# The steps of an attention pair at other slots of the schedule

## The chip, the cores and the metric

The kernel runs on one core of a Trainium2 chip. A core has five engines that each work through their own queue in order: TensorE (PE in the profile; PEld is its loading of weights), VectorE (DVE), ScalarE (ACT), GpSimd (POOL) and SyncE (SP). SP and POOL issue most of the DMAs. The metric is the time of one execution on the device in microseconds; below, the median of three runs is used, and one further execution was profiled.

## The reference

Two layers, each a mixer with two branches over 256 tokens of 2048 channels, in float32. What matters here is the attention branch and what runs beside it:

```python
proj = h @ w_in                                  # one input projection, cut into nine parts
y_conv = conv_branch(c_a, c_glu, c_gate, ...) @ w_proj_conv    # GLU, causal depthwise conv of width 31, LayerNorm, gates
q  = rmsnorm((rmsnorm(q_down) @ w_uq))           # 16 heads of 128 + 64 (rotary)
kv = rmsnorm(kv_down) @ w_ukv                    # 16 heads: 128 of key, 128 of value
s  = q @ k.T * scale, masked by chunks of 64     # per head, 256 x 256
o  = softmax(s) @ v
y  = sigmoid(g_conv) * y_conv + sigmoid(g_mla) * (o * silu(gate)) @ w_proj_mla
x  = x + y @ w_out
```

## The kernel before

**Products and slots.** Every large product is cut into blocks of at most 512 output columns, and a block runs over its weight pieces of 256 rows. One piece is a *slot*: twelve matmuls (two token halves, two row groups, three terms). Three terms, because a float32 weight is split into a high part, rounded by a cast on ACT (`split_hi`, tile `hi`), and a low part, the difference, taken on DVE (`split_lo`, tile `lo`). Both are made some slots ahead: before the matmuls of slot j come the cast for slot j+3 and the difference for slot j+2. There are 4 buffers for high parts, 3 for low parts, 5 for raw weights, which SP loads in order.

**The order of the work.** Each engine's instructions are issued in the order of the Python program; nothing is reordered. After the matmuls of a slot, `background` (L243) advances a slot counter, then issues the steps that are due (`at_slot(ahead, f, vec, act)` files a step `ahead` slots from now), then *fill* work, and last what the steps appended to `late`. A step's work therefore stands in the DVE and ACT queues between the weight splits of neighbouring slots, and its matmuls stand between the matmuls of neighbouring slots.

**The planner's budget.** Fill is the depthwise convolution, one *tap* after another, on DVE. A tap is either two multiply-adds of 128x256, one for each half (charged 0.81 by the planner), or one add of 128x512 (charged 0.62) if ACT has scaled the input before (`assist`, when ACT's own budget is over 0.8). Each slot earns for DVE what the planner's estimate of the slot leaves beside the low part: 1.55 for a slot of 512 columns, 1.18 for one of 384. Charges of the due steps are taken off, and as long as the balance is above zero a tap is issued; a negative balance is carried on, a positive one is not:

```python
        slot = 12 * (n / 2400 + 0.0133) - 0.04
        for e, split_us in (("vec", KS * n / 960 + 0.06), ("act", KS * n / 1066 + 0.04)):
            budget[e] = min(budget[e], 0.0) + slot - split_us
```

These are the planner's numbers, fixed in the code; they decide only where a tap stands.

**A round.** The attention works on pairs of heads, eight to a layer. For pair b a layer runs two slots of `uq` (384 columns, queries), two of `ukv` (512, keys and values) and eight of another block: a `glu` block (input of the convolution) for pairs 0 to 4, a `cgate` block for pairs 5 and 6. So there is a round of twelve slots from the end of one `ukv` product to the end of the next. Below, *round b* is the one after pair b's `ukv`, and its slots are counted 1 to 12: 1 to 8 are `glu` or `cgate`, 9 and 10 `uq` of the next pair, 11 and 12 its `ukv`.

**The steps of a pair** (`attention`, L667, steps filed at L812 to L825) are counted in slots from the end of its `ukv`, over almost three rounds, so that three pairs are at work in each round. In order: `stats` (DVE, 14 small operations: the RMSNorm factors), `scale_k` (DVE, four operations; then eight DMAs on POOL park the query and key rows in DRAM, `turn_d<-qk`), `back_in("qk")` (two POOL DMAs fetch them back, `qk<-turn_d`), `blockwise` (DVE, two transposes of 32x32 blocks), `split_nope` (three ACT operations; differences on DVE a slot later), `split_rope` (six ACT casts; four differences on DVE a slot later), `scores` (16 matmuls, tile `s`), `maxima` (DVE, after a copy on ACT; tiles `sx`, `nb`), `exponentials` (ACT, into tile `pr`; then four POOL DMAs park it, `turn_d<-pr`), `back_in("p")` (one POOL DMA, `pr<-turn_d`), `turn_p` (DVE: reciprocal, transpose), `split_p` (a cast on ACT, and `late` a difference on DVE, tile `pv`), `values` (12 matmuls, tile `o_ps`), `outputs` (a copy on ACT, `o_sb`). Within a slot, steps are issued in the order in which they were filed, the older pair first.

**Beside them in each round.** The block that ends with slot 8 is evacuated in slot 9: for `glu` two sigmoids on ACT and, as `late`, two products on DVE (tile `su`; then eight POOL DMAs `turn_d<-su`, two fetches four slots on, two transposes `u_t` eight slots on, which open the next block of taps); for `cgate` two silus on ACT and eight parks. The `uq` block is evacuated in slot 11, `ukv` in slot 1 of the next round. `ukv` in slot 11 writes the two PSUM tiles that the `glu` or `cgate` block held, so it can't begin before that evacuation is done. After the last tap of a block comes one more sum (`s1c`).

Of the kernel before, what the change touches and what calls it, by code (L numbers as in the profile page):

```python
# [63 lines left out]
EVAC_AT = 1  # L64
FETCH_AT, TURNED_AT = 4, 8

STATS_AT, SCALE_AT, QK_BACK_AT, QK_TURN_AT, NOPE_AT, ROPE_AT, SCORES_AT = 2, 3, 6, 11, 12, 14, 17
MAX_AT, EXP_AT, P_BACK_AT, P_TURN_AT, P_SPLIT_AT, VALUES_AT, O_AT = 18, 19, 23, 28, 30, 32, 34

REVOLUTION_PIECES = 6  # L70

# [1249 lines left out]
```

## Time and profile before

| | us |
|---|---|
| median of 3 runs (lowest, highest) | 1892.09 (1891.77, 1892.33) |
| the profiled execution, whole time | 1891.51 |
| its span, first to last instruction | 1889.7 |
| PE busy | 1881.9 (100%) |
| DVE busy | 1601.2 (85%) |
| ACT busy | 1331.5 (70%) |
| POOL busy | 392.9 (21%) |

The granted TensorE clock is 1.000. How to read the rows below: a row of instructions has the start and the length in us, the engine, the operation, the tile written and the tiles read, shapes, and how many instructions were merged into the row; in brackets stands how long the engine had been idle before it and what ended that. Instructions of one engine overlap a little at their ends, so a cost in a queue is best taken from start to start. Busy PE is no sign of PE at its peak; a stall of PE shows as a longer distance between matmuls that stand in the same order.

### The profile page before, as it was taken

What the parts mean: (1) busy time and instruction counts of PE and PEld (TensorE: products, weight loads), DVE (VectorE), ACT (ScalarE), POOL (GpSimd) and SP (SyncE); (2) the same over time, 40 slices, a digit from 0 to 9 for tenths busy, and PEclk for the clock granted to TensorE, in tenths of its full rate; (3) what the DMA queues carried; (4) which work ended last, traced back from release to release, by engine and by line L of the source; (5) the groups of instructions that cost most, each with busy time, mean ns of one, the idle gap of its engine ahead of it and who ended that gap; (6) DMA issues with size and microseconds to landing.
All of it is one profiled execution on the core that took longest, in us unless ns stands there. A gap on an engine that the chain in (4) does not pass through costs nothing.

```text
span 1889.7 us, 27378 instructions
## 1 busy us (share of the span) xinstructions
PE 1881.9 (100%) x8744; PEld 1589.4 (84%) x8744; DVE 1601.2 (85%) x2623; ACT 1331.5 (70%) x2350; POOL 392.9 (21%) x734
## 2 busy tenths in 40 slices
PE   9999999999999999999999999999999999999999
PEld 8988888888888888888899888888888888888887
DVE  6899998899999998765679898888999999985654
ACT  7677878878787866544557688688887878474442
POOL 1043433332200000121211443343322000001200
PEclk9999999999999999999999999999999999999999
DMA  9678778776765566677866877787767555666764
GB/s 321 218 251 275 258 236 272 256 256 225 229 210 192 187 218 217 216 236 258 281 209 216 263 263 243 260 266 241 257 228 237 199 189 195 225 213 215 237 224 164
DMA packets 137232, 441.91 MB, mean 234 GB/s; under 512 B 23296, under 2 KB 27136, under 8 KB 137088
## 3 DMA queue, kind: packets, MB, share of 16 engines
q1 hardware_dynamic: 104256, 358.84, 56.5%
q0 software_dynamic: 31968, 80.26, 13.4%
q8 instruction: 68, 1.11, 0.2%
q10 hardware_dynamic: 864, 1.07, 0.2%
q14 instruction: 76, 0.62, 0.1%
HBM read 397.61 MB, written 42.47 MB: 233 GB/s over the span
## 4 chain that ended last, share of the span: by engine, by line
PE 97%; DVE 2%; ACT 1%; DMA 0%; issue 0%; POOL 0%; ACTq 0%; DVEq 0%
PE acc L127 94%; PE s L127 2%; PE o_ps L127 1%; DVE lo L127 1%; DVE v_t L127 0%; DMA x_in<-in_xT 0%; ACT hi L127 0%; ACT tap L127 0%; DVE qk L127 0%; DMA turn_d<-pr 0%; PE tp L127 0%; ACT qk L127 0%; DVE rsq_t L127 0%; DVE ym L127 0%; ACT junk L127 0%
## 5 line engine op out<-in xcount | busy, mean ns | idle before, releaser
L127 ACT CAST hi<-raw 128x1024 fp32r<-128x1024 f32 (+3 forms) x689 | 699.5, 1022 | 411.7 <-PE acc L127 351.7
L127 DVE TENSOR_TENSOR lo<-raw,hi 128x1024 fp32r<-128x1024 f32 (+3 forms) x689 | 811.4, 1181 | 207.8 <-PE acc L127 164.7
L127 PE MATMUL acc<-hi,hT 128*128 128x512 f32 (+2 forms) x1728 | 419.8, 382 | 0.0
L127 PEld LDWEIGHTS acc<-hi,hT 128*128 128x128 f32 x1728 | 319.8, 188 | 59.1
L127 ACT ACTIVATE tap<-u_t,cst 128x256 f32<-128x256 f32 x598 | 260.9, 500 | 14.6 <-DVE v_t L127 13.6
L127 PE MATMUL acc<-hi,h_hi 128*128 128x512 f32 (+2 forms) x864 | 261.3, 384 | 1.1 <-ACT hi L127 1.1
L127 PE MATMUL acc<-hi,h_lo 128*128 128x512 f32 (+2 forms) x864 | 260.1, 382 | 0.0
L127 PE MATMUL acc<-lo,h_hi 128*128 128x512 f32 (+2 forms) x864 | 229.8, 382 | 0.0
L127 PE MATMUL acc<-lo,hT 128*128 128x512 f32 (+2 forms) x864 | 229.3, 382 | 0.0
L127 DVE TENSOR_TENSOR v_t<-v_t,tap 128x512 f32<-128x512 f32 x299 | 205.3, 687 | 10.1
L127 PEld LDWEIGHTS acc<-hi,h_lo 128*128 128x128 f32 x864 | 161.2, 188 | 30.2
L127 PEld LDWEIGHTS acc<-hi,h_hi 128*128 128x128 f32 x864 | 160.4, 188 | 31.0 <-ACT hi L127 1.5
L127 PEld LDWEIGHTS acc<-lo,h_hi 128*128 128x128 f32 x864 | 160.9, 188 | 30.0
L127 PEld LDWEIGHTS acc<-lo,hT 128*128 128x128 f32 x864 | 160.6, 188 | 29.9
L127 POOL DMA_DIRECT2D turn_d<-gate x176 | 95.6, 551 | 321.5 <-DVE gate L127 278.0
L127 DVE SCALAR_TENSOR_TENSOR v_t<-u_t,cst,v_t 128x256 f32<-128x256 f32 x362 | 155.4, 480 | 3.0
L127 POOL DMA_DIRECT2D turned<-turn_d x82 | 45.9, 560 | 519.6 <-DVE v_t L127 317.3
L127 PE MATMUL acc<-hi,oT 128*128 128x512 f32 x512 | 128.1, 390 | 0.0
L127 PE MATMUL acc<-hi,yT 128*128 128x512 f32 x512 | 128.0, 389 | 0.0
L127 PE MATMUL acc<-hi,ycT 128*128 128x512 f32 x512 | 127.8, 389 | 0.0
L127 PE MATMUL acc<-hi,qkc 128*128 128x512 f32 (+1 forms) x512 | 119.0, 364 | 0.2
L127 PEld LDWEIGHTS acc<-hi,oT 128*128 128x128 f32 x512 | 96.1, 188 | 20.1
(171 smaller groups left out, 2139.8 us busy)
## 6 DMA issues: line engine op xcount, KB each, us to landing
raw<-in_win SPq DMA_DIRECT2D x383, 512.0 KB, 4.2
raw<-in_wpm SPq DMA_DIRECT2D x64, 512.0 KB, 3.2
raw<-in_wpc SPq DMA_DIRECT2D x64, 512.0 KB, 4.0
raw<-in_wo SPq DMA_DIRECT2D x64, 512.0 KB, 4.3
raw<-in_wukv SPq DMA_DIRECT2D x32, 512.0 KB, 5.2
turned<-turn_d POOLq DMA_DIRECT2D x50, 256.0 KB, 4.5
raw<-in_win SPq DMA_DIRECT2D x32, 384.0 KB, 4.4
raw<-in_wuq SPq DMA_DIRECT2D x32, 384.0 KB, 3.0
```

Source lines behind the costliest of these rows:

```text
L127: ins = getattr(self.engine, name)(*a, **k)
```

## The change

Only two lines of constants change: the slots of a pair's steps.

```diff
-STATS_AT, SCALE_AT, QK_BACK_AT, QK_TURN_AT, NOPE_AT, ROPE_AT, SCORES_AT = 2, 3, 6, 11, 12, 14, 17
-MAX_AT, EXP_AT, P_BACK_AT, P_TURN_AT, P_SPLIT_AT, VALUES_AT, O_AT = 18, 19, 23, 28, 30, 32, 34
+STATS_AT, SCALE_AT, QK_BACK_AT, QK_TURN_AT, NOPE_AT, ROPE_AT, SCORES_AT = 3, 5, 8, 11, 12, 15, 18
+MAX_AT, EXP_AT, P_BACK_AT, P_TURN_AT, P_SPLIT_AT, VALUES_AT, O_AT = 19, 20, 24, 29, 30, 32, 35
```

In slots of a round (counts above 12 and 24 fall into the next rounds):

| step | slot before | slot after |
|---|---|---|
| `stats` | 2 | 3 |
| `scale_k` and 8 parks | 3 | 5 |
| fetch of the rows, 2 DMAs | 6 | 8 |
| `blockwise`, `split_nope` | 11, 12 | the same |
| `split_rope`, its differences | 2, 3 | 3, 4 |
| `scores` | after 5 | after 6 |
| `maxima` | 6 | 7 |
| `exponentials` and 4 parks | 7 | 8 |
| fetch of `pr` | 11 | 12 |
| `turn_p` | 4 | 5 |
| `split_p`, `values` | 6, 8 | the same |
| `outputs` | 10 | 11 |

No instruction is added or removed; the orders of the queues of PE, DVE, ACT and POOL change, and with the charges the slots in which the planner puts taps.

## The prediction

> **What bounds the kernel now.** I read the page's first part, then PE's waits, then the chain of waits, then the timeline of one attention round, engine by engine. PE is busy throughout, its waits are small, and the chain (start, length, what) runs along PE's products with 16 score matmuls in each round:
>
> ```profile
> PE   1881.9 (100%) x8744; PEld 1589.4 (84%) x8744; DVE 1601.2 (85%) x2623; ACT 1331.5 (70%) x2350; POOL 392.9 (21%) x734
> ...
> PE acc L127 <- ACT hi L127: 1.1, 1, 1.1
> PE s L127 <- DVE qk_t L127: 0.7, 1, 0.7
> ...
> 208.50 1.89 PE s L127 x16
> 243.18 1.89 PE s L127 x16
> 383.12 1.89 PE s L127 x16
> 1147.17 1.89 PE s L127 x16
> 1181.88 0.04 DVEq L127
> 1217.60 2.23 PE s L127 x16
> 1322.80 1.89 PE s L127 x16
> ```
>
> From 208.50 to 243.18 a round takes 34.68 us; I take that as the unstalled round. The four rounds to 383.12 take 139.94, 1.22 more than 4 x 34.68; the five from 1147.17 to 1322.80 take 175.63, 2.23 more. So all stalls of both attention stages come to 3.45 us, and that is all a better order of these steps could give back. But at 1181.88 the chain leaves PE and returns only at 1217.60: for a whole round something other than PE set the pace. It is a loop of DVE and ACT, seen in the timelines of that round (a window with the busy time of PE, PEld, DVE, ACT, POOL; then DVE, then ACT, then PE):
>
> ```profile
> 1158.60:1193.30 34.70, 34.70 (x174) 29.96 (x173) 31.03 (x63) 28.06 (x65) 13.39 (x26) 1.00 0.77 253
> ...
> 1179.88 1.78 DVE L127 TENSOR_TENSOR qk_t<-qk,qk_t 64x256 fp32r<-64x256 f32 x4
> 1188.43 0.16 DVE L127 TENSOR_TENSOR nb<-nb,rs_p 128x4 f32<-128x4 f32 x1
> 1188.51 0.95 DVE L127 TENSOR_TENSOR pv<-pr,pv 128x768 fp32r<-128x768 f32 x1
> 1189.38 1.82 DVE L127 TENSOR_TENSOR lo<-raw,hi 128x768 fp32r<-128x768 f32 x2
> 1191.12 1.41 DVE L127 TENSOR_TENSOR v_t<-v_t,tap 128x512 f32<-128x512 f32 x2
> 1194.23 1.23 DVE L127 TENSOR_TENSOR lo<-raw,hi 128x1024 fp32r<-128x1024 f32 x1 [1.71 <-ACT hi L127]
> 1196.98 0.88 DVE L127 SCALAR_TENSOR_TENSOR su<-acc,rinv_x,su 128x256 f32<-128x256 f32 x2 [1.51 <-ACT su L127]
> 1198.90 1.67 DVE L127 SCALAR_TENSOR_TENSOR v_t<-u_t,cst,v_t 128x256 f32<-128x256 f32 x4
> 1200.60 0.69 DVE L127 TENSOR_TENSOR s1c<-s1c,v_t 128x512 f32<-128x512 f32 x1
> 1202.35 1.83 DVE L127 STREAM_TRANSPOSE qk<-qk 128x768 f32<-128x768 f32 x2
> ...
> 1189.81 1.28 ACT L127 ACT_TABLE_LOAD   x1 [3.30 <-DVE pv L127]
> 1193.07 0.20 ACT L127 ACTIVATION_READ_ACCUMULATOR pr<-s,nb,rs_p 128x1 f32 x1
> 1193.16 1.99 ACT L127 CAST hi<-raw 128x1024 fp32r<-128x1024 f32 x2
> 1195.17 1.28 ACT L127 ACT_TABLE_LOAD   x1
> 1196.47 0.84 ACT L127 ACTIVATE su<-acc,rinv_x 128x256 f32<-128x256 f32 x2
> 1229.04 0.19 ACT L127 ACTIVATION_READ_ACCUMULATOR pr<-s,nb,rs_p 128x1 f32 x1
> ...
> 1197.61 2.09 PE L127 MATMUL acc<-hi,qkc 128*128 128x512 f32 x8
> ```
>
> The reader is to see a ring. DVE's maxima (`nb`) and the difference `pv` release ACT's table load and exponentials; they end at E = 1193.07 + 0.20 = 1193.27. Behind them in ACT's queue stand two casts (1.99), a table load (1.28) and the sigmoids `su`; the first product on DVE is done at about 1197.45, and PE's slot 11, which needs that PSUM tile, starts at 1197.61, E + 4.3. Then DVE works its queue through to the next maxima without a long wait. From E to the next E (1229.23) are 35.96 us; 0.69 of them is the `s1c` sum, which falls into few rounds, so the ring takes 35.27 where PE needs 34.68. It is as good as closed already. DVE is busy 31.03 of 34.70, and most of its idle time is the two waits for ACT just behind the maxima (1.71 and 1.51). What is put ahead of the maxima lengthens the ring; what stands behind them, while ACT works, is free.
>
> **The change part by part.** Seen from the ring, most moves cost nothing: `stats`, `scale_k`, the rotary differences (1.78), `turn_p` and the maxima all stood between the transposes of `qk` and the maxima, and still do. Four things differ.
>
> (a) The difference `pv` (slot 6) used to stand behind the maxima (slot 6) with the exponentials waiting for it; now it stands ahead of them (slot 7). ACT waited for it then, so: nothing.
>
> (b) The maxima stand a slot later, so the low part for slot 9, first half of the pair at 1189.38 (0.87 from start to start), is now ahead of them: +0.87.
>
> (c) Taps. The charges for DVE in slots 1 to 8 were 1.95, 2.2, 2.75, 1.0, 0.8, 2.4, 0, 0, and each slot earns 1.55. A late round of the first layer leaves slot 12 at about -0.45 and goes -0.85, -1.50, -2.70, -2.14, -1.39, -2.24, -0.69 and at slot 8 +0.86: two taps there, two in slot 10. The pair at 1191.12 (1.41) is slot 8's: behind the maxima, free. Now they are 1.95, 0, 2.2, 1.65, 2.9, 0.9, 1.5, 0, and the same walk gives slot 1 -1.0 and slot 2, where no step is left, +0.5: a tap there, ahead of the maxima. It has no ACT help (ACT's budget recovers only in slots 5 to 7), so it costs half of the 1.67 at 1198.90: +0.84. Carried on round by round, the walk gives one tap in slot 2 in rounds 2 to 6 of the first layer; in the second layer one in round 2, two (+1.67) in rounds 3, 5 and 6, and one with `s1c` (0.84 + 0.69) in round 4. Slot 10 gets one or two adds in place of multiply-adds: -0.13 each.
>
> (d) The exponentials stand a slot later, so one cast (half of 1.99) fewer lies between them and `su`: -0.98.
>
> Ring on DVE and ACT alone: 35.27 + 0.87 + 0.84 - 0.98 - 0.13 = 35.87 with one tap, 35.27 + 0.87 + 1.67 - 0.98 - 0.27 = 36.56 with two.
>
> (e) POOL's queue. The rows' fetch moves from slot 6 to slot 8, and there the older pair's four parks of `pr` are filed ahead of it. Before, it waited only for its own parks:
>
> ```profile
> 1185.78 0.57 POOL L127 DMA_DIRECT2D qk<-turn_d  x1 [1.50 <-DMA turn_d<-qk]
> 1189.27 0.56 POOL L127 DMA_DIRECT2D qk<-turn_d  x1 [2.92 <-DMA turn_d<-qk]
> 1193.56 2.20 POOL L127 DMA_DIRECT2D turn_d<-pr  x4 [3.73 <-ACT pr L127]
> ...
> qk<-turn_d POOLq DMA_DIRECT2D x32, 384.0 KB, 5.4
> ...
> DMA to landing us min/median/max: 2.1/3.6/6.9
> ```
>
> Now: E + 0.3, parks 2.20, so the two fetches go out at E + 2.5 and E + 3.1 and land (5.4) at E + 7.9 and E + 8.5. DVE reaches the two transposes (half of 1.83 each) at about E + 7.3 (before: 1202.35, E + 9.1 with 0.69 of `s1c`; now 1.11 earlier by (d) and slot 10) and ends them at E + 9.7 where it would have ended at E + 9.1: +0.6. The ends: 2.1 to landing makes it 0; 6.9 makes the transposes end at E + 11.2: +2.1. I take 0.6, by the median of this very transfer. The ring is then 36.5 with one tap, 37.2 with two; against 34.68 PE stalls 1.8 or 2.5 a round.
>
> [...]
>
> The rest lies beside other work. `scores` moves from a point where the rotary differences end at 1181.66, right at the matmuls, to one slot later, with `scale_k` no longer ahead of them but a low part and a tap or two more. A slot, on average 34.68 / 12 = 2.9 us, is as long as a low part and two taps (1.23 and 1.67), and the four scalings are gone from there besides; so the differences are done in time, and the 3.45 us of old stalls vanish. `outputs` now queues behind the `uq` evacuation; its 0.59 falls into ACT's waiting for the transposes, and were that gone would cost at most 0.59 of ACT, whose 28.06 has room. The fetch of `pr` has five slots to `turn_p` as before. `su`'s parks stand behind the fetch on POOL and have four slots. SP's order is untouched.
>
> **The sum.** In rounds 2 to 6 exponentials stand before an evacuation that slot 11 waits for.
>
> ```profile
> 222.88 0.87 DVE L127 SCALAR_TENSOR_TENSOR su<-acc,rinv_x,su 128x256 f32<-128x256 f32 x2 [1.52 <-ACT su L127]
> ...
> 223.94 2.01 PE L127 MATMUL acc<-hi,qkc 128*128 128x512 f32 x8
> ...
> L127 ACT ACTIVATE gate<-acc,rinv_x 128x512 f32<-128x512 f32 x32 | 20.5, 684 | 0.4 <-DVE v_t L127 0.2
> L127 DVE STREAM_TRANSPOSE u_t<-turned 128x256 f32<-128x256 f32 x32 | 12.2, 420 | 0.0
> L127 ACT COPY o_sb<-o_ps 128x512 f32<-128x512 f32 x16 | 9.4, 588 | 0.0
> ```
>
> Round 2: the first product (half of 0.87) is ready at about 223.35, 0.6 before PE wants it. E comes later by 0.87 + 0.84 and about 0.9 carried over from round 1 (an estimate: that round's own (b) and (c), less DVE's idle time), 2.6; less 0.98 and 0.6 leaves 1.0. Rounds 3 and 4: 1.8 each. Round 5: a `cgate` block, freed by one silu on ACT (0.68) instead of half of `su`'s 0.84 on ACT and then half of 0.87 on DVE, hence about 0.2 to 0.3 earlier: 1.5. Round 6: besides, no `u_t` transposes (2 x 0.42, overlapping, about 0.7), which leaves about 0.4 less again: 1.1. First layer 7.2. Second layer: 1.0, 2.5, 2.4, 2.2, 1.8: 9.9. Together 17.1, less the old 3.45: +13.7. The profiled execution took 1891.5, so 1905.2; the median lies 0.6 above it: 1906. With fetches that never hold DVE, ten rounds lose 0.6 each: 1900. With the worst landing they gain 1.5 each: 1921.
>
> **The rivals.** (1) Faster: the scores stop waiting for the rotary differences and no new wait appears. Place: slot 11. It decides if the exponentials end less than 0.98 + 0.6, about 1.6 us, later, that is if (b) and (c) are swallowed by DVE's 3.2 us of waits. For it: the 0.7 wait of `s` is real. Against: those waits stand behind the maxima, the new work ahead. Time: 1892.1 - 3.45 = 1888.6. (2) No change: the lateness does not add up over rounds, because PE's own slack of 0.6 and the shorter casts take it; each layer loses about what it wins. Against it: the ring of 35.27 shows no slack to recover in. 1890 to 1895. (3) POOL decides: the fetches, back to back behind the parks and beside weight loads, land at 6.9 or later. For it: DMA share 0.77 in the window. 1913 to 1921 or above.
>
> **How the numbers follow.** The forecast, a ring of 36 to 37 us, has 0.72, with a range of its own of 1898 to 1913. Rival 3 has 0.12, rival 2 0.11, rival 1 0.05. Leaving out rival 1, most of rival 2 and the far end of rival 3 gives 1894 to 1919. A measurement of this kernel tells about 0.2% (3.8 us) from no change; rival 1's 3.45 hardly reaches it. Faster 0.05, within it 0.12, slower 0.83.
>
> **What would show it.** In the changed kernel the chain of waits should run through DVE and ACT in rounds 2 to 6 of both layers; score groups 36 to 37.5 us apart; slot 11's first matmul waiting for DVE `su` (in `cgate` rounds ACT `gate`) and the wait of `s` for `qk_t` gone; POOL's `qk` fetch waiting for its parks no longer; DVE's transposes of `qk` waiting for a DMA by about 0.6; a tap of multiply-adds between the `vl` and `stats` work. Wrong would make it: rounds that stay at 34.7 (the ring is not closed), or a fetch that lands far from 5.4.

## The result, and the profile after

The changed kernel takes 1913.62 us (median of four runs, 1913.13 to 1914.98) beside 1892.21 for the kernel before in the same series. The ratio is 1.0113, with a 95% interval of 1.0097 to 1.0129: slower by 21 us. The profiled execution took 1913.8, its span 1911.7, 22.0 more than before, and PE is busy 1888.2 of it. The planner also made three taps of the changed kernel in the other form, two multiply-adds in place of an add that ACT helps: DVE runs 2626 instructions where it ran 2623, ACT 2344 where it ran 2350. So a few instructions do change with the slots.

The waits of the changed kernel (in us: in total, how many, the longest), PE's first, then what DVE waits for ahead of the transposes of `qk` and ahead of the products `su`:

```profile
PE acc L127 <- DVE su L127: 7.4, 6, 2.3
PE acc L127 <- ACT gate L127: 4.9, 4, 1.6
PE acc L127 <- DVE lo L127: 2.2, 4, 0.9
PE acc L127 <- ACT hi L127: 2.0, 1, 2.0
PE s L127 <- DVE qk_t L127: 0.7, 3, 0.2
PE mu L127 <- DVE s1c L127: 0.2, 1, 0.2
...
DVE su L127 <- ACT su L127: 20.7, 8, 4.3
DVE qk L127 <- DMA turn_d<-gate: 13.4, 4, 3.9
DVE qk L127 <- DMA qk<-turn_d: 7.4, 7, 2.7
```

The first six lines come to 17.4 us, where the kernel before had 1.8 (1.1 and 0.7). The 2.0 for `hi` stands at the start of the program, as the 1.1 did before. Most of the rest is slot 11, waiting for the evacuation that frees its PSUM tiles, by `su` in `glu` rounds and by `gate` in `cgate` rounds. The last two lines are new and come to 20.8: DVE stands still because the rows of `qk` have not come back. (The tile in the name of a releasing DMA is the one seen last; the rows themselves are `qk<-turn_d`.)

Round 2 of the first layer in the chain of waits (start, length, what):

```profile
221.28 3.05 PE acc L127 x18
224.33 0.94 ACT hi L127
225.27 0.02 issue
225.29 1.28 ACT L127
226.57 0.01 issue
226.58 0.48 ACT su L127
227.06 0.02 issue
227.09 0.49 DVE su L127
227.58 0.14 issue
227.72 23.64 PE acc L127 x96
```

This is the ring of the prediction, now closed around PE: exponentials end at 224.33, then one cast (0.94), the table load, one sigmoid, one product, and slot 11 at 227.72. The timeline of the same round, POOL, DVE and PE:

```profile
224.62 2.18 POOL L127 DMA_DIRECT2D turn_d<-pr  x4 [4.09 <-ACT pr L127]
226.79 1.12 POOL L127 DMA_DIRECT2D qk<-turn_d  x2
...
222.74 0.68 DVE L127 TENSOR_TENSOR v_t<-v_t,tap 128x512 f32<-128x512 f32 x1
227.09 0.87 DVE L127 SCALAR_TENSOR_TENSOR su<-acc,rinv_x,su 128x256 f32<-128x256 f32 x2 [3.66 <-ACT su L127]
...
227.72 3.65 PE L127 MATMUL acc<-hi,qkc 128*128 128x512 f32 x8 [2.27 <-DVE su L127]
```

POOL parks `pr` 0.3 after the exponentials and fetches the rows at once behind it, as foreseen. DVE idles 3.66 behind the maxima (1.52 before at this place). And the eight matmuls of slot 11 take 3.65, where the same eight took 2.01 before: after the stall PE ran at half its pace for a while, 1.6 us on top of the 2.27. The second layer has the same at 1176.67 (3.63). The named waits (+15.6, of which 0.9 is that at the start of the program) and the two slow stretches (+3.3) make 18.9 of the 22.0; the rest is in shorter distances between matmuls.

### The profile page after: what moved, and what is told of

It is laid out like the page before. It is cut to its first block, busy times and chain, and to the rows that moved or that the text cites. A ratio compares the mean times of both kernels' runs of the same rounds, so it can differ in the third digit from the quotient of the medians.

```text
span 1911.7 us, 27327 instructions
## 1 busy us (share of the span) xinstructions
PE 1888.2 (99%) x8744; PEld 1590.3 (83%) x8744; DVE 1601.7 (84%) x2626; ACT 1324.5 (69%) x2344; POOL 392.2 (21%) x734
## 4 chain that ended last, share of the span: by engine, by line
PE 87%; DVE 5%; issue 2%; ACT 2%; DMA 2%; POOL 1%; ACTq 0%; DVEq 0%
PE acc L127 85%; DVE lo L127 2%; DVE v_t L127 1%; PE s L127 1%; PE o_ps L127 1%; DVE qk_t L127 1%; ACT hi L127 1%; DMA qk<-turn_d 1%; ACT L127 1%; POOL turn_d L127 0%; DMA x_in<-in_xT 0%; DVE qk L127 0%; ACT pr L127 0%; DMA turn_d<-gate 0%; DMA turn_d<-su 0%
## 5 line engine op out<-in xcount | busy, mean ns | idle before, releaser
L127 POOL DMA_DIRECT2D turn_d<-qk x128 | 69.9, 554 | 242.5 <-DVE qk L127 167.9
```

The source lines that it names most:

```text
L127: ins = getattr(self.engine, name)(*a, **k)
```

## The experiments

Every kernel below computes all of the reference unless something else is said. E is the end of a pair's exponentials, as in the prediction.

**One kernel with three moves, one with eight.** First the change was cut in two: the kernel before with the first three moves (factors, scaling, fetch), and the changed kernel with those three taken back.

```diff
 e3_first_three, against the kernel before
-STATS_AT, SCALE_AT, QK_BACK_AT, ... = 2, 3, 6, 11, 12, 14, 17
+STATS_AT, SCALE_AT, QK_BACK_AT, ... = 3, 5, 8, 11, 12, 14, 17
 e4_other_eight, against the changed kernel
-STATS_AT, SCALE_AT, QK_BACK_AT, ... = 3, 5, 8, 11, 12, 15, 18
+STATS_AT, SCALE_AT, QK_BACK_AT, ... = 2, 3, 6, 11, 12, 15, 18
```

> Only the first three moves (factors in the third slot, scaling and its parks in the fifth, rows fetched back in the eighth); all else as before. Taps move to slot 2 by the planner's walk. Theory R: ring 35.27 + 0.84 to 1.67 = 36.1 to 36.9, nothing else changed in it, so as bad as the whole change or nearly: 1904 to 1914. Theory Q: the exponentials and their parks are a slot earlier than the fetch here, so the fetch stands half as long behind them: 1900 to 1906.

> Only the other eight moves (rotary split, scores, maxima, exponentials, fetch of the probabilities, their turn, the outputs a slot later); factors, scaling and the rows' fetch in the second, third and sixth slot as before. By the planner's walk no tap stands ahead of the maxima in rounds 2 to 5. Theory R: ring 35.27 + 0.87 - 0.98 = 35.2 as before, and the scores no longer wait for the rotary differences: 1890 to 1895. Theory Q: the fetch is back ahead of the exponentials' parks, so the same, 1890 to 1895; the two halves together tell whether the loss belongs to the first three moves at all. If it were the later place of the exponentials, right before the evacuation of slot 9, this half would be as slow as the change: 1905 to 1914.

The first took 1911.98 (1906.85 to 1912.01), ratio 1.0097 (1.0082 to 1.0112). The second took 1889.38 (1888.92 to 1890.85, ten runs), ratio 0.9985 (0.9976 to 0.9994): faster than both kernels. So the whole loss sits in the three moves at the front, and the other eight win 2.9 us by themselves (the kernel before took 1892.28 in that series).

**Taps without any step moved.** To see what the order of the taps costs, only a charge was moved in the kernel before: the factors are still issued in slot 2, and the planner is told of them in slot 3. It then finds slot 2 free and puts a tap there, ahead of the maxima.

```diff
-            at_slot(STATS_AT, stats, 2.2)
+            at_slot(3, lambda: None, 2.2)
+            at_slot(STATS_AT, stats)
```

> The kernel before with only the planner's charge of the factors (2.2) filed in slot 3 instead of slot 2; every step stays in its old slot. By the planner's walk one multiply-add tap of about 0.84 us then moves from behind the maxima (slot 8) to slot 2, ahead of them; the count of taps is the same. Theory R: the ring goes from 35.27 to about 36.1, each of the ten rounds 2 to 6 stalls 1 to 1.4 us more: 1900 to 1905. Theory Q: nothing on POOL moves, so no change, 1891 to 1894.

1900.25 (1899.32 to 1902.11), ratio 1.0042 (1.0028 to 1.0056): 8 us for a few taps at another place in a queue. One of them changed its form besides (DVE has one instruction more than before, ACT two fewer).

**The changed kernel with the taps back.** The reverse: all steps where the change put them, the charges filed in slot 2.

```diff
-            at_slot(STATS_AT, stats, 2.2)
-            at_slot(SCALE_AT, scale_k, 1.1)
+            at_slot(2, lambda: None, 3.3)
+            at_slot(STATS_AT, stats)
+            at_slot(SCALE_AT, scale_k)
```

> The changed kernel with the planner's charges of the factors and the scaling (2.2 + 1.1) both filed in slot 2; the steps themselves stay where the change put them. By the planner's walk no tap then stands between slot 1 and slot 7 of rounds 2 to 6, the taps go to slots 8 to 10. Theory R (a ring of DVE and ACT: what stands ahead of the maxima sets the pace): the ring falls from about 36 to 37 us to 35.27 + 0.87 - 0.98 = 35.2 in rounds with a glu block, and most of the loss goes: 1894 to 1900, what is left sitting in rounds 5 and 6 (cgate). Theory Q (POOL's queue: the fetch of the rows behind the parks of the exponentials sets the pace): taps do not matter, 1908 or more.

1907.11 (1904.15 to 1910.82), ratio 1.0079 (1.0064 to 1.0094). Neither range holds it; it lies just under the bound of theory Q, not near that of the ring: only 6.5 us go with the taps. With them gone DVE waits longer for the rows. Its waits ahead of the transposes of `qk`:

```profile
DVE qk L127 <- DMA turn_d<-gate: 18.6, 6, 4.9
DVE qk L127 <- DMA qk<-turn_d: 14.1, 11, 3.8
```

That is 32.7 us in place of 20.8: part of what the taps no longer cost is spent waiting for the rows instead.

**The fetch one slot earlier, and the taps alone.** Two kernels part the remaining suspects. In e5 only the fetch moves back, from slot 8 to 7, so that on POOL it is filed ahead of the older pair's parks of `pr`. In e6 scaling and fetch go back to slots 3 and 6 and the factors stay in slot 3, which keeps the taps early.

```diff
 e5_rows_back_seventh, against the changed kernel
-STATS_AT, SCALE_AT, QK_BACK_AT, ... = 3, 5, 8, 11, 12, 15, 18
+STATS_AT, SCALE_AT, QK_BACK_AT, ... = 3, 5, 7, 11, 12, 15, 18
 e6_taps_only, against the changed kernel
-STATS_AT, SCALE_AT, QK_BACK_AT, ... = 3, 5, 8, 11, 12, 15, 18
+STATS_AT, SCALE_AT, QK_BACK_AT, ... = 3, 3, 6, 11, 12, 15, 18
```

> The changed kernel with the rows' fetch alone moved back one slot, from the eighth to the seventh (where POOL has not yet been given the older pair's parks of pr); tap order as in the changed kernel. Theory F (most of what the taps do not explain is the fetch's place on POOL, behind pr's four parks in the rounds of cgate): the transposes of qk stop waiting by some 2 us in rounds 5 to 7 of either layer, 1903 to 1908. Theory S (the fetch is late because scaling and its own parks are late, so that its slot decides nothing): 1911 to 1915.

> The changed kernel with scaling back in the third slot and the rows' fetch back in the sixth; the factors stay in the third, so that the convolution's taps stay in the second slot, ahead of the maxima. The four kernels with and without each part then stand side by side: both 1913.6, no tap in the second slot 1907.1, neither 1889.4. Theory A (the two parts add): 1889.4 + (1913.6 - 1907.1) = 1896, 1894 to 1898, and no wait of qk's transposes for a fetch in the rounds of cgate. Theory T (the taps alone make the loop too long and the fetch only adds where there is slack): 1900 to 1906.

e5: 1901.99 (1899.62 to 1903.37), ratio 1.0050 (1.0035 to 1.0065), better than either theory said. One slot of the fetch is worth 11.6 us. e6: 1901.14 (1900.67 to 1901.56), ratio 1.0046 (1.0029 to 1.0063). It is theory T by its number, and the two parts do not add: each hides some of the other. The two kernels end within a microsecond of each other, so with the fetch in slot 7 nothing is left of its part.

What the taps do is seen best where nothing else is moved. The last read-out of the exponentials on ACT, in rounds 2 and 5 of the first layer, in the kernel of the other eight moves, then in e6:

```profile
220.65 0.19 ACT L127 ACTIVATION_READ_ACCUMULATOR pr<-s,nb,rs_p 128x1 f32 x1
...
324.40 0.19 ACT L127 ACTIVATION_READ_ACCUMULATOR pr<-s,nb,rs_p 128x1 f32 x1
```

```profile
221.98 0.20 ACT L127 ACTIVATION_READ_ACCUMULATOR pr<-s,nb,rs_p 128x1 f32 x1
...
329.24 0.19 ACT L127 ACTIVATION_READ_ACCUMULATOR pr<-s,nb,rs_p 128x1 f32 x1
```

Three rounds lie between: 34.58 us each without the tap and 35.75 with it. The first is PE's own pace (the score groups of that kernel, e4, stand 34.69 apart in these rounds), the second is the ring.

**The fetch alone, and scaling alone.** Three more kernels start from the tap orders of e4 and e1. There no tap stands ahead of the maxima in rounds 2 to 5; one add is left in round 6 of each layer, and one tap in round 7 of the second. e9 is the kernel of the other eight moves with the fetch in slot 8 and nothing else. e10 and e11 are e1 with the fetch in slot 7 and in slot 6; factors and scaling stay late in both.

```diff
 e9_rows_back_alone, against e4
-STATS_AT, SCALE_AT, QK_BACK_AT, ... = 2, 3, 6, 11, 12, 15, 18
+STATS_AT, SCALE_AT, QK_BACK_AT, ... = 2, 3, 8, 11, 12, 15, 18
 e10_no_tap_seventh, against e1
-STATS_AT, SCALE_AT, QK_BACK_AT, ... = 3, 5, 8, 11, 12, 15, 18
+STATS_AT, SCALE_AT, QK_BACK_AT, ... = 3, 5, 7, 11, 12, 15, 18
 e11_no_tap_sixth, against e1
-STATS_AT, SCALE_AT, QK_BACK_AT, ... = 3, 5, 8, 11, 12, 15, 18
+STATS_AT, SCALE_AT, QK_BACK_AT, ... = 3, 5, 6, 11, 12, 15, 18
```

> The kernel with only the other eight moves (1889.4), and the rows' fetch alone moved from the sixth slot to the eighth; factors, scaling and taps stay early. Theory F (the eighth slot itself costs, since POOL has the older pair's four parks of pr ahead of the fetch there): as with the same tap order and all three moves, 1907.1: 1904 to 1910, with the transposes of qk waiting for the fetch. Theory S (late scaling and late own parks are what makes the fetch late): 1889 to 1892.

> The changed kernel with no tap ahead of the maxima (1907.1), and the rows' fetch in the seventh slot instead of the eighth; factors in the third and scaling in the fifth as in the change. Theory F (taps and the eighth slot are the whole loss): 1889 to 1892. Theory S (late scaling holds the rows back as well): 1895 to 1905.

> As the run before it, with the rows' fetch in the sixth slot: scaling's own parks of 4.4 us then stand right ahead of the fetch on POOL. Theory F: 1889 to 1892, the same as in the seventh slot. Theory S: 1895 to 1905, the same too, since the fetch waits for its own parks whichever slot it has.

| tap ahead of the maxima in rounds 2 to 5 | fetch in slot 6 or 7 | fetch in slot 8 |
|---|---|---|
| no | e4 1889.38, e10 1889.53, e11 1889.60 | e9 1906.05, e1 1907.11 |
| yes | e6 1901.14, e5 1901.99 | the change 1913.62 |

All three came out as theory F had it. The fetch in slot 8 alone costs 16.7 us (e9, ratio 1.0070, 1.0055 to 1.0085). Late factors and late scaling cost nothing, whichever slot the fetch has: e10 and e11 (ratios 0.9986, 0.9977 to 0.9996, and 0.9988, 0.9979 to 0.9998) are as fast as e4. These two things are the loss: 11.8 us for the taps, 16.7 for the fetch, 24.2 together, since in places one wait covers the other. The part of the taps holds a little more than their place: 13 taps are two multiply-adds in e6 that are one add in e4.

The difference between slots 7 and 8 is one queue. POOL in round 5 of e9 and of e10:

```profile
326.99 2.18 POOL L127 DMA_DIRECT2D turn_d<-pr  x4 [9.87 <-ACT pr L127]
329.15 1.12 POOL L127 DMA_DIRECT2D qk<-turn_d  x2
```

```profile
322.81 0.57 POOL L127 DMA_DIRECT2D qk<-turn_d  x1 [1.52 <-DMA turn_d<-qk]
325.50 0.56 POOL L127 DMA_DIRECT2D qk<-turn_d  x1 [2.12 <-DMA turn_d<-qk]
326.06 2.20 POOL L127 DMA_DIRECT2D turn_d<-pr  x4
```

In e9 POOL idles for 9.87 us, with the fetch behind four parks whose data do not exist yet. In e10 the fetch stands ahead of them and waits only for its own parks; its first half goes out 6.3 us earlier, of which 1.6 is that the round itself is earlier (E at 325.1 against 326.7). DVE's waits for the rows, e9 and then e10:

```profile
DVE qk L127 <- DMA qk<-turn_d: 13.9, 12, 2.8
DVE qk L127 <- DMA turn_d<-gate: 11.2, 5, 4.6
```

```profile
DVE qk L127 <- DMA turn_d<-gate: 0.8, 1, 0.8
DVE qk L127 <- DMA qk<-turn_d: 0.4, 1, 0.4
```

**Where the fetch hurts.** In `glu` rounds of the changed kernel the rows come about when DVE wants them (waits of at most 0.56 in rounds 2 to 4). In `cgate` rounds they don't (2.68 to 3.85 in rounds 5 to 7). DVE in round 5 of the changed kernel, then the same stretch of e6, whose fetch is early:

```profile
336.65 1.23 DVE L127 TENSOR_TENSOR lo<-raw,hi 128x1024 fp32r<-128x1024 f32 x1 [0.71 <-ACT hi L127]
341.27 1.84 DVE L127 STREAM_TRANSPOSE qk<-qk 128x768 f32<-128x768 f32 x2 [3.39 <-DMA turn_d<-gate]
```

```profile
333.92 1.22 DVE L127 TENSOR_TENSOR lo<-raw,hi 128x1024 fp32r<-128x1024 f32 x1 [0.70 <-ACT hi L127]
335.06 1.83 DVE L127 STREAM_TRANSPOSE qk<-qk 128x768 f32<-128x768 f32 x2
```

Two things meet. DVE is there sooner: in e6 the transposes start 5.6 us after E in this round and 7.3 after E in round 2 (E at 329.4 and 222.2). And the fetch takes longer. Its time from issue to landing in the changed kernel, in a `glu` round (296 to 310 us) and in this one (332 to 346):

```profile
qk<-turn_d POOLq DMA_DIRECT2D x2, 384.0 KB, 3.9
...
qk<-turn_d POOLq DMA_DIRECT2D x2, 384.0 KB, 6.6
```

Eight parks of 64 KB (`turn_d<-gate`) follow the fetch on POOL in `cgate` rounds, where `glu` rounds have eight of 32 KB. In e12 they are issued three slots later for three blocks of each layer:

```diff
-            keep["parked"][c][t] = park(g, 512, park_d)
+            def parked():
+                keep["parked"][c][t] = park(g, 512, park_d)
+            if c < 3:
+                at_slot(3, parked)
+            else:
+                parked()
```

> The changed kernel with the eight parks of the cgate rows (8 x 64 KB) three slots later on POOL for the first three cgate blocks of each layer, so that they no longer go out right behind the fetch of qk's rows; nothing else moves. Theory G (those parks share the DMA engines with the fetch and are why it lands 6.1 to 6.6 us after its issue in cgate rounds and 3.9 to 5.3 in glu rounds): it lands in 4 to 5.3, the six cgate rounds lose 1 to 1.7 us less each, 1904 to 1909. Theory W (the landing is set by the weight loads, or the round has another floor): 6 us and more as before, 1912 to 1915.

1911.36 (1906.77 to 1915.87), ratio 1.0097 (1.0075 to 1.0119), nearer to theory W, and not sharp. In round 5, POOL and DVE show

```profile
334.02 1.12 POOL L127 DMA_DIRECT2D qk<-turn_d  x2
338.87 3.82 POOL L127 DMA_DIRECT2D turn_d<-gate  x7
...
339.65 2.03 DVE L127 STREAM_TRANSPOSE qk<-qk 128x768 f32<-128x768 f32 x2 [2.38 <-DMA qk<-turn_d]
```

so the parks are out of the way and the wait is 2.38 instead of 3.39; but over the six rounds the transposes end 10.1 to 11.2 us after E, beside 10.4 to 11.9 in the changed kernel, and the spread of the runs covers the gain. The parks are at most a small part. What makes this fetch slower in `cgate` rounds stays open.

**The slow matmuls after a stall.** In e7 six spare matmuls stand ahead of the stalled place in round 2 of each layer, to keep PE from idling there. They add work that the reference doesn't have.

```diff
+                if i == 3:
+                    spare = tp_p.tile([P, 512], F32, tag="tp", name="spare")
+                    for n in range(6):
+                        pe.matmul(spare, h_hi[:, 0, :P], h_hi[:, 0:2, :], start=n == 0, stop=n == 5)
```

> The changed kernel with six spare matmuls of 512 columns (6 x 0.227 = 1.36 us) put on TensorE ahead of the place at which it stands idle for 2.4 us in the second round of either layer; they add 1.36 us of matmul and cut the idle time by as much. Theory C (the eight matmuls at half pace come from an idle time of over some 2 us): they run at 0.227 again, 1.6 us gained in either layer, 1909.5 to 1911. Theory N (half pace has another cause, or the loop sets the end and takes the gain back): 1912.5 to 1915.

```profile
223.55 1.55 PE L127 MATMUL spare<-h_hi 128*128 128x512 f32 x6
225.58 2.08 PE L127 MATMUL acc<-hi,qkc 128*128 128x512 f32 x8 [0.48 <-DVE su L127]
...
1247.92 2.09 PE L127 MATMUL acc<-hi,qkc 128*128 128x512 f32 x8 [2.47 <-DVE su L127]
```

The half pace is gone from both places (2.08 here, 1.98 at 1174.13 in the second layer), and yet the kernel takes 1914.75 (1912.38 to 1917.05), ratio 1.0119 (1.0104 to 1.0134), no less than the changed kernel. Theory N holds for the time: PE's longest wait is now 2.47 in a later round, and as in the ring's account, what PE gains at one place it waits for at another. So the 3.3 us named above do not look like a loss of their own: taking them away saved nothing here.

**A last attempt on the fastest kernel.** In e8 the `u_t` transposes, too, go behind the maxima:

```diff
-                turn(u, 256, lambda z: conv(b) if t == T - 1 else None, us[b][:, :, at : at + P], (0.4, 0.0))
+                turn(u, 256, lambda z: conv(b) if t == T - 1 else None, us[b][:, :, at : at + P], (0.4, 0.0), at=11)
```

> The kernel with only the other eight moves (1889.4), and in it the block transposes of the glu rows three slots later, so that they come behind the maxima on DVE instead of ahead of them (0.65 us of DVE out of the stretch from scores to exponentials). Theory L (the loop still sets the end in those rounds): 1886 to 1888.5. Theory P (TensorE is the bound there and the loop has room): 1889 to 1890.5, no difference.

1889.74 (1889.17 to 1891.96, ten runs), ratio 0.9989 (0.9979 to 0.9998), in the range of theory P. But this kernel does not test a shorter ring in most rounds. With the charge of the transposes gone to a later slot, the planner put a tap ahead of the maxima in rounds 3 to 5 of the first layer and 2 to 4 of the second, about 0.8 where the transposes took 0.7. DVE between the transposes of `qk` in round 2 and the maxima of round 3, where e4 has no tap:

```profile
231.25 0.88 DVE L127 SCALAR_TENSOR_TENSOR v_t<-u_t,cst,v_t 128x256 f32<-128x256 f32 x2
```

That a shorter ring has nothing to win is therefore read from e4 itself: its score groups stand 34.69 apart in every round from 2 to 6 of both layers, at PE's own pace.

## Why the prediction was right, and where it was not

The time lies inside the range and the sign is right, 7.6 us above the number. The forecast gave its own case 1898 to 1913; the result is 0.6 above that, just where the rival of POOL begins; the range held because that rival had been given a part in it. Both mechanisms are in the result: 11.8 for the taps and then 12.5 for the fetch, or 16.7 for the fetch and then 7.6 for the rest. Of the 7.6 us, 1.1 is the kernel with early taps and an early fetch (1901.1 where the sum has 1900), and 6.5 is the fetch (12.5 where it has 6).

*The ring, and steps (a) to (d): right.* The ring with one tap and no fetch in the way was worked out as 35.87; e6, which is just that, runs at 35.75; with two taps it was 36.56, and e6 has 36.36 from round 2 to round 3 of the second layer, where two stand. The tap's +0.84 stands in the stretch from the transposes to E, which is 25.8 us in seven of the eight `glu` rounds of e9 (25.8 to 26.2 in e4, which has room), 26.6 in e6, and 27.3 to 27.4 there where two taps, or one and `s1c`, stand in it. The planner's walk missed one tap: ahead of the maxima of round 2 of the second layer stand two. The step "with fetches that never hold DVE: 1900" was the lower end; e6 and e5 measured 1901.1 and 1902.0. That the 3.45 of old stalls vanish came out as 2.9 in e4. That late factors, late scaling and their parks cost nothing is shown by e10 and e11.

*Step (e): right in its mechanism, half of what it should have been.* POOL did what was written: parks at E + 0.3, fetches at E + 2.5 and E + 3.0. The price was one 0.6 for ten rounds alike, 6 us. From e6 to the changed kernel it is 12.5 (11.6 from e5, whose taps stand where those of the changed kernel do). Against e6, the transposes of the changed kernel end at most 0.4 later after E in rounds 2 to 4, which is less than said; 1.3 and 1.8 later in round 1 of the two layers; and 2.9 to 4.4 later in rounds 5 to 7, of which the last had no place in the sum. From one E to the next, round 1 then loses 1.3 and 1.4, rounds 5 and 6 1.3 to 1.8, and round 7 3.1 and 3.3 (e6 has some slack in these rounds). What failed is that DVE's arrival and the fetch's landing were taken as one pair of numbers for all rounds (7.3 after E, and 5.4): in `cgate` rounds DVE arrives at 5.6 and the fetch takes 6.1 to 7.4 (the middle of its two halves). In the sum those rounds had been given a discount, because a `cgate` block is freed sooner; the same earliness makes DVE meet the missing rows. The row of 5.4, taken for every round, was too kind to `cgate` rounds, as the 6.6 above beside the 3.9 of a `glu` round shows. The row that gave the ends, 2.1 and 6.9, has the parks of 96 KB among the fetches; the fetches alone took 3.9 to 6.9 in the kernel before, so the lower end stays where it was, as a landing after 3.9 holds nobody in that working either.

*Round 2's stall of 1.0: too small.* It measured 2.27, and 1.6 of slow matmuls came on top. E came 5.2 us later (224.33 against 219.17), where 2.6 was put down; PE, itself 1.5 later there (225.45 against 223.94), hid part of it. e4 has E at 220.85 and e6 at 222.17. So 1.7 of it comes with the other eight moves and their later scores; 1.3 comes with the taps, and 2.2 with the fetch in rounds 0 and 1, which step (e) was not applied to (0.5 and 0.3 of these two are a later start of the products at the head of the program).

*What would show it.* The chain through ACT and DVE, the wait of slot 11 for `su` and `gate`, the wait of the transposes for a DMA, the taps ahead of the maxima: all are there. From E to E rounds 2 to 6 take 35.8 to 37.5; the score groups, whose places PE's own stalls move, stand 34.7 to 38.8 apart. The wait of `s` for `qk_t` was to be gone and is not: it is three short ones, 0.7 in all, as much as before. "The fetch waits for its parks no longer" holds everywhere but in round 0 of either layer and, for one half of the fetch, in round 1 of the first (0.95). Rival 1, that the scores stop waiting and nothing new waits, is what the eight moves do by themselves; the first three moves lose over eight times as much. Rival 2 fell with the result, and e2 says why: no slack took up the taps, which alone cost 8 us.

## What to carry to other kernels

In a queue that is served in order, look at what a moved step is put behind, not only at what it needs: here a fetch was filed behind four transfers whose data did not exist yet while the queue idled, and in the changed kernel one slot earlier gave 11.6 us back. If a planner fills gaps, moving a step's charge moves the fill, and where the fill lands relative to the one chain that sets the pace decides its price. And price a wait for each kind of round on its own: the consumer's arrival and the transfer's landing, each from that round's rows, since the rounds in which the consumer is early are the ones that pay.

## What the runs showed of the hardware

PE's half pace after a stall was not expected. In the changed kernel the eight matmuls of 512 columns behind waits of 2.27 and 2.26 us took 3.65 and 3.63 us instead of 2.01. It is not a matter of the length of the wait alone: in e7 a wait of 2.47 (at 1247.92 above) was followed by full pace, and in e12 one of 2.10 by half pace:

```profile
1173.96 3.51 PE L127 MATMUL acc<-hi,qkc 128*128 128x512 f32 x8 [2.10 <-DVE su L127]
```

The mean granted clock of these spans is 0.998 for the changed kernel, 1.000 for e7 and 0.999 for e12. The mean hides what happens. Here are stretches of 3.41 us (start and end, length, busy time of PE, PEld, DVE, ACT and POOL, the granted clock, DMA share, GB/s), two of the changed kernel and then two of e7:

```profile
224.28:227.69 3.41, 1.17 (x7) 0.85 (x6) 0.60 (x2) 3.38 (x6) 3.07 (x6) 1.00 0.89 299
227.69:231.10 3.41, 3.38 (x8) 2.76 (x9) 3.37 (x6) 3.38 (x12) 2.49 (x6) 0.50 0.89 273
...
1243.37:1246.78 3.41, 2.08 (x12) 1.76 (x11) 0.31 (x1) 3.39 (x7) 1.95 (x4) 1.00 0.86 270
1246.78:1250.19 3.41, 2.27 (x10) 1.90 (x11) 2.90 (x6) 3.40 (x8) 3.41 (x8) 1.00 0.91 281
```

The clock falls to 0.50 at 227.69 and is back at 1.00 after 3.41 us. The next such stretch of this kernel begins at 1176.60, which is 948.91 us or 278 times 3.41 us (3.413) later. The trace's records of the clock begin at 5.83, 227.69, 231.11, 1176.60, 1180.01 and 1910.46 us in this execution, 65, 1, 277, 1 and 214 such steps apart: here the clock changed on a grid of that step. Ahead of the two stretches PE was busy for 1.17 and 1.22 us of a step, and for 1.3 us of the 3.41 ahead of the slow matmuls of e12. At the start of the changed kernel, a border of the grid at 9.24 cuts a wait of 2.05 (8.67 to 10.72) in two; PE is busy for 2.84 and 1.93 us of the two steps, and the clock stays at 1.00. In e7 the border of the two stretches above, 1246.78, lies within the wait of 2.47; PE is busy for 2.08 and 2.27 us of them, and the clock stays at 1.00. That it matters how a stall lies across the grid is a reading of these five stalls; no run tested it.
